# The raw projection weights issued on ScalarE's DMA queue in place of SP's, after the first 11 chunks

## The chip, the cores and the metric

One core of a Trainium2 chip. The metric is the device time of one execution in microseconds (us), the median of several runs. Instructions of five engines run side by side: PE (TensorE, matmuls; PEld is its weight load), DVE (VectorE), ACT (ScalarE), POOL (GpSimd) and SP (SyncE, which only issues DMAs). ACT and POOL can issue DMAs too. An engine takes its instructions strictly in the order in which they were written for it, so one that waits holds all behind it.

## The reference

A two-layer backbone over 2048 latent and 256 context tokens of width 1024, in fp32:

```python
xn = _rms_norm(x, g_norm) * (1 + sc) + sh          # sc, sh: silu(c) @ w_ada + b_ada
(au, av, az, bq, bk, bv, bz, cq, ck, cv, co, cz, cg) = _split_proj(xn @ w_in)
y_a = _gmlp_branch(au, av, az, w_s, b_s)           # chunks of 128 tokens
y_b = attention(q=bq, k=bk, v=bv) * silu(bz)       # 8 heads, 2 kv heads, rms norm and rope
y_c = sigmoid(co) * rms_norm(mlstm(cq, ck, cv, cg), both directions) * silu(cz)
x = x + gt * (concat([y_a, y_b, y_c]) @ w_out)
```

Context tokens go through the same weights. After the second layer a last RMSNorm follows.

## The kernel before

Tokens are tiled by 128: 18 tiles, 2 of context and 16 of latents. Each layer has a projection phase (`proj_phase`), an attention phase (`attn_phase`) and an output phase (`out_phase`). In the profile the projections run from 0 to about 890 us and from about 1740 to 2690 us.

**Projections.** The 18 tiles are taken in three macros of six. For each macro seven column groups (c1, c3, c2, a1, a2, b1, b2) are computed; for each group and tile, 8 contraction chunks times 3 matmuls (a weight and an input are each split in a high and a low part) add up in one PSUM bank: 24 matmuls. The normalized, split input of a tile is its `xn` (L465 to L487). After a tile's matmuls a post-processing generator of the group (`post_c1` to `post_b2`) takes the bank, mostly by ScalarE first.

**Weights.** A chunk is 128 rows of one group: 3 x 7 x 8 = 168 chunks in a layer. `wload` (L942) loads a chunk's raw fp32 into one of 3 buffers `raw`; `split_w` (L197) makes the split weight `w` from it: ScalarE copies (L199) and VectorE subtracts (L200), or, for every fourth chunk, GpSimd does both (L202, L203). `w` has 11 buffers, 8 for the group at work and 3 ahead. A `raw` buffer comes free with the subtraction; a `w` buffer with the last matmul that reads it.

**Queues.** `ld` (L50) issues on SP's queue (L53). All loads and nearly all stores go there; ScalarE issues the stores of c1 and c3 to scratch (L495, L518). Each DMA raises one of 8 semaphores, which all DMAs of SP and ACT take in turn, and a DMA waits until the one before it on its semaphore has landed.

**Modulations and tables.** The modulations of layer 1 and the gates `gt` are made during layer 0 as filler (`mod_job`): 64 blocks of `w_ada` go into 3 buffers `mst`, and VectorE adds them into `mkv` (L401, L403: two instructions a block); PE sums over partitions (L434, L443). The rope tables `tab` are loaded in `rope_mul`. Both loads stand under `with tc.issue_after(lastw[0])`: it puts each instruction that is issued on the same engine as `lastw[0]`, the raw load issued last, behind that load.

**mLSTM.** In the last macro of a layer the mLSTM's jobs run beside the projections (`ml_state`, `ml_out`): chains of small loads (`mkv`, `mst`, `xt<-snm`, `msc`), a few instructions, and stores (`sst`, `sy`), all on SP's queue.

**Order.** A scheduler orders each engine's instructions by a simulated timeline; the order in which the code traces them is the priority. So an instruction that may start earlier can be put ahead of others on its engine.

Of the kernel before, what the change touches and what calls it, by code (L numbers as in the profile page):

```python
# [35 lines left out]
def hybrid_kernel(ctx: ExitStack, tc: tile.TileContext, x, c, ctxt, c_ctx, w_ada, b_ada, g_norm, w_in, w_s, b_s,  # L36
                  gq, gk, b_gates, g_head, w_out, g_final, rope, out):
    nc = tc.nc
# [12 lines left out]
    def ld(dst, src):  # L51

        r = nc.sync.dma_start(dst, src)  # L53
        if gate[0] is not None:
            tc.add_manual_dep(r.ins, gate[0].name,
                              mybir.DependencyInfo(mybir.DependencyClass.NoSync, mybir.DependencyReason.DATA),
                              reason="order of the loads")
        return r

    def nm(s):  # L60
        uid[0] += 1
        return f"{s}_{uid[0]}"
# [242 lines left out]
    def proj_phase(l):  # L305
        with ExitStack() as st:
# [624 lines left out]
            for mi in range(NM):  # L931
                for gn, cols in groups:
                    for k in range(KC):
                        src, o = [], 0
# [4 lines left out]
            wt, wraw, lastw = [], [], [None]  # L939
            freed = [0]  # L940

            def wload():  # L942
                while len(wraw) < len(chunks) and len(wraw) < len(wt) + 3:
                    raw = rawp.tile([P, 512], F32, tag="raw", name=nm("raw"))
                    for (a, o, w) in chunks[len(wraw)][0]:
                        lastw[0] = ld(raw[:, o:o + w], a).ins
                    wraw.append(raw)

            def wtick(most=2):
                for _ in range(most):  # L950
                    j = len(wt)
                    if j >= len(chunks) or j >= freed[0] + 11:
                        break
                    wt.append(split_w(wraw[j], wring(), chunks[j][1], chunks[j][2] % 4 != 1))
                    wload()

            xgens = [make_xn(i, halves=first) for i in macros[0][:AHEAD]]
            if first:
                silu_prep()
                rT = mod_rows(0)  # L960
                mod_load(0, 0)
                for gen in xgens:
                    next(gen)
                    next(gen)
                mod_first(0, 0, rT)
                wload()
                mod_load(0, 1)
                for gen in xgens:
                    next(gen)
                    next(gen)  # L970
                wtick(4)
                mod_first(0, 1, rT)
                for gen in xgens:
                    run_all(gen)
                wtick(12)
                layer_params(0, k2(), k1(P)[0:4])
            else:
                with tc.high_priority(offset=140):
                    wload()
                    wtick(12)  # L980
                    for gen in xgens:
                        run_all(gen)
            for mi, mac in enumerate(macros):
                for gi, (gn, cols) in enumerate(groups):
# [8 lines left out]
                    for ii, i in enumerate(mac):  # L993
                        full = not (last and i < NCT)
                        ml = mi == NM - 1 and (gi >= 3 or gi == 2 and ii >= 1)
                        if i in todo:
                            acc = pacc()
                            c0, w = (0, n) if full or gn == "c3" else (256, 256)
# [291 lines left out]
```

## Time and profile before

| | |
|---|---|
| median of 3 runs | 3673.63 us (3672.63 to 3673.88) |
| the profiled execution | 3684.58 us, its span 3682.9 us |
| PE busy | 3582.6 us, 97% of the span |
| DVE, ACT, POOL busy | 2556.9 us (69%), 1942.0 us (53%), 1892.3 us (51%) |
| DMA moved | 359.21 MB, mean 98 GB/s |
| chain that ended last, by engine | PE 69%, DMA 6%, DVE 4%, POOL 3%, issue 2%, SP's queue 2%, ACT 2% |

The last row follows the end of the program back to what released each step. SP has no busy time in the profile, since issuing is not counted; its DMA issues stand in the timeline as SPq, and those of ScalarE as ACTq.

### The profile page before, as it was taken

How to read it: one execution, taken by the hardware profiler on the slowest of the kernel's cores; microseconds unless marked ns; L12 is line 12 of the kernel's file. 1: busy time of each engine (PE TensorE's matmuls, PEld its weight loads, DVE VectorE, ACT ScalarE, POOL GpSimd, SP SyncE). 2: the span in 40 equal slices, each digit the busy share in tenths (PEclk: the TensorE clock that was granted, in tenths of full speed). 3: DMA queues.
4: the chain of work that ended last, by engine and by line, in shares of the span. 5: the costliest groups of instructions: out<-in, count | busy, mean ns of one | idle time of the engine just before them, and what ended most of it. 6: DMA issues, size and time to landing. Idle time of an engine off the chain costs nothing.

```text
span 3682.9 us, 58371 instructions
## 1 busy us (share of the span) xinstructions
PE 3582.6 (97%) x19405; PEld 2937.3 (80%) x19405; DVE 2556.9 (69%) x6341; ACT 1942.0 (53%) x3409; POOL 1892.3 (51%) x2448
## 2 busy tenths in 40 slices
PE   8999999998999999999999999999999999999999
PEld 4877778776888888887788788877778888888787
DVE  4676664778888888887324636466888888888754
ACT  4223243334878788786114432432377877777621
POOL 2241342454777777776322524244557777777610
PEclk9999999999999999999999999999999999999999
DMA  7456455576001011002545553557720101100143
GB/s 216 137 138 175 138 129 136 159 194 156 25 28 37 17 35 43 24 12 95 175 121 151 132 148 83 141 145 180 174 57 18 31 27 35 35 24 10 58 148 113
DMA packets 531690, 359.21 MB, mean 98 GB/s; under 512 B 297274, under 2 KB 432178, under 8 KB 531388
## 3 DMA queue, kind: packets, MB, share of 16 engines
q1 hardware_dynamic: 518172, 336.05, 33.8%
q10 hardware_dynamic: 10368, 9.52, 0.8%
q0 software_dynamic: 2848, 9.91, 0.7%
q8 instruction: 154, 2.52, 0.3%
q14 instruction: 148, 1.21, 0.1%
HBM read 269.56 MB, written 85.76 MB: 96 GB/s over the span
## 4 chain that ended last, share of the span: by engine, by line
PE 69%; DMA 6%; DVE 4%; POOL 3%; issue 2%; SPq 2%; ACT 2%; DVEq 0%; POOLq 0%; ACTq 0%
PE acc L209 20%; PE m L1131 14%; PE acc L1096 14%; PE tr L1113 9%; PE x L209 6%; PE x L1113 4%; SPq L53 2%; DMA raw<-in_w_in_dram 1%; DMA xt<-snm 1%; DMA mkv<-sc 1%; DMA tab<-in_rope_dram 1%; DVE w L200 1%; DVE e L1098 1%; PE tr L476 0%; POOL pT L1120 0%
## 5 line engine op out<-in xcount | busy, mean ns | idle before, releaser
L209 PE MATMUL acc<-w,xn 128*128 128x512 f32 (+2 forms) x4728 | 1096.5, 385 | 5.3 <-POOL w L203 1.7
L209 PEld LDWEIGHTS acc<-w,xn 128*128 128x128 f32 x4728 | 844.2, 191 | 182.8 <-issue 5.4
L1098 DVE TENSOR_SCALAR_CACHE_REDUCE e<-acc,rqall 128x512 f32<-128x512 f32 (+1 forms) x1296 | 858.1, 690 | 144.4 <-PE acc L1096 76.6
L1131 PE MATMUL m<-pT,vst 128*128 128x512 f32 (+1 forms) x2336 | 775.3, 415 | 4.8 <-POOL pT L1120 4.0
L1096 PE MATMUL acc<-kst,qs 128*128 128x512 f32 (+1 forms) x2592 | 744.5, 385 | 11.6 <-DVE e L1098 10.0
L1120 POOL TENSOR_TENSOR pT<-pf,pT 128x512 fp32r<-128x512 f32 (+1 forms) x564 | 730.5, 1302 | 29.7
L1104 ACT ACTIVATE e<-e,nmx 128x2304 f32<-128x2304 f32 (+1 forms) x272 | 578.5, 2127 | 61.4 <-DVE nmx L1103 60.7
L1119 POOL TENSOR_SCALAR pT<-pf 128x512 fp32r<-128x512 f32 (+1 forms) x564 | 356.8, 636 | 338.5 <-ACT pf L1118 332.9
L1096 PEld LDWEIGHTS acc<-kst,qs 128*128 128x128 f32 x2592 | 447.4, 189 | 92.1 <-DVE e L1098 21.7
L1131 PEld LDWEIGHTS m<-pT,vst 128*128 128x128 f32 x2336 | 411.7, 189 | 65.6 <-POOL pT L1120 8.6
L1113 PE MATMUL tr<-ident,e 128*128 128x128 f32 x3084 | 456.9, 273 | 3.0 <-DVE pT L1123 2.1
L1113 PEld LDWEIGHTS tr<-ident,e 128*128 128x128 f32 x3084 | 375.1, 141 | 79.1 <-DVE pT L1123 4.0
L200 DVE TENSOR_TENSOR w<-raw,w 128x512 fp32r<-128x512 f32 (+1 forms) x276 | 205.5, 755 | 184.0 <-ACT w L199 182.3
L199 ACT CAST w<-raw 128x512 fp32r<-128x512 f32 (+1 forms) x276 | 161.6, 595 | 299.0 <-DMA raw<-in_w_in_dram 265.1
L1123 DVE TENSOR_TENSOR pT<-tr,pT 128x512 fp32r<-128x512 f32 x405 | 274.2, 683 | 59.5 <-ACT pT L1122 58.4
L209 PE MATMUL acc<-w,xs 128*128 128x512 f32 x1224 | 294.2, 398 | 1.7 <-DVE xs L249 1.3
L1122 ACT CAST pT<-tr 128x512 fp32r<-128x512 f32 x405 | 234.4, 587 | 95.2 <-PE tr L1113 79.8
L209 PEld LDWEIGHTS acc<-w,xs 128*128 128x128 f32 x1224 | 230.9, 189 | 58.3 <-DVE xs L249 1.7
L209 PE MATMUL x<-w,xn 128*128 128x512 f32 (+1 forms) x1128 | 263.3, 379 | 10.4 <-DVE w L200 6.0
L1118 ACT COPY pf<-tr 128x512 f32<-128x512 f32 (+1 forms) x372 | 214.5, 584 | 87.1 <-PE tr L1113 77.8
L202 POOL TENSOR_SCALAR w<-raw 128x512 fp32r<-128x512 f32 (+1 forms) x92 | 65.5, 712 | 361.7 <-PE acc L209 158.7
L209 PEld LDWEIGHTS x<-w,xn 128*128 128x128 f32 x1128 | 200.1, 190 | 54.8 <-DVE w L200 8.9
(282 smaller groups left out, 4402.9 us busy)
## 6 DMA issues: line engine op xcount, KB each, us to landing
raw<-in_w_in_dram SPq DMA_DIRECT2D x240, 256.0 KB, 3.1
raw<-in_w_in_dram SPq DMA_DIRECT2D x144, 128.0 KB, 2.4
mkv<-sc SPq DMA_DIRECT2D x68, 258.0 KB, 4.0
xt<-snm SPq DMA_DIRECT2D x68, 256.0 KB, 4.5
yr<-sy SPq DMA_DIRECT2D x34, 512.0 KB, 6.5
mst<-in_w_ada_dram SPq DMA_DIRECT2D x64, 256.0 KB, 3.7
qd<-sq SPq DMA_DIRECT2D x128, 128.0 KB, 2.8
xres<-xnew POOLq DMA_DIRECT2D x18, 512.0 KB, 5.2
```

What stands on the lines that cost most here:

```text
L200: V.tensor_tensor(wt[:, 1, :n], raw[:, :n], wt[:, 0, :n].bitcast(F32), op=ALU.subtract)
L209: T.matmul(acc[:, :n], xs[:, a, k, :], ws[k][:, b, c0:c0 + n], start=(k == 0 and j == 0), stop=(k == KC - 1 and j == 2))
L1096: T.matmul(acc[:, 0:w], u['qs'][:, r, j * P:(j + 1) * P], kf[:, c0:c0 + w], start=(r == 0), stop=(r == 1))
L1098: V.tensor_scalar(e[:, c0:c0 + w], acc[:, 0:w], rqall[:, u['tiles'][j], u['h']:u['h'] + 1], None, op0=ALU.mult, op1=ALU.max, accum_out=mx[ ...
L1104: A.activation(e[:, 0:nk], e[:, 0:nk], AF.Exp, bias=nmx, scale=1.0, accum_out=u['den'][:, j:j + 1])
L1113: T.transpose(tr[:, j * P:(j + 1) * P], u['e'][j][:, s * P:(s + 1) * P], ident)
L1118: A.copy(pf[:, 0:w], tr[:, 0:w])
L1119: G.tensor_scalar(pt_[:, 0, 0:w], pf[:, 0:w], 1.0, 0.0, op0=ALU.mult, op1=ALU.add)
L1120: G.tensor_tensor(pt_[:, 1, 0:w], pf[:, 0:w], pt_[:, 0, 0:w].bitcast(F32), op=ALU.subtract)
L1122: A.copy(pt_[:, 0, 0:w], tr[:, 0:w])
L1123: V.tensor_tensor(pt_[:, 1, 0:w], tr[:, 0:w], pt_[:, 0, 0:w].bitcast(F32), op=ALU.subtract)
L1131: T.matmul(u['o'][:, 0:w], vst[u['g']][:, s, :], pt_[:, r, 0:w], start=(s == 0 and r == 0), stop=(s == u['nk'] - 1 and r == 1))
```

## The change

From the 12th chunk of each layer on, the raw weights are issued by ScalarE:

```diff
             def wload():
                 while len(wraw) < len(chunks) and len(wraw) < len(wt) + 3:
+
+                    q = ld if len(wraw) < 11 else nc.scalar.dma_start
                     raw = rawp.tile([P, 512], F32, tag="raw", name=nm("raw"))
                     for (a, o, w) in chunks[len(wraw)][0]:
-                        lastw[0] = ld(raw[:, o:o + w], a).ins
+                        lastw[0] = q(raw[:, o:o + w], a).ins
                     wraw.append(raw)
```

Line numbers behind this place grow by 2, and the moved loads have L948. `lastw[0]` is now an instruction of ScalarE for all but the start, while the loads under `issue_after` stay on SP.

**VectorE at the start of layer 0**, behind the first half of the first three tiles' `xn` (xn_324, xn_333, xn_342). `mst` are blocks of `w_ada` for the filler, `mkv` its sums, `w` the split weights of the first groups:

```order
 L487 TENSOR_TENSOR xn_333<-xt_330,xn_333 128x512
 L487 TENSOR_TENSOR xn_342<-xt_339,xn_342 128x512
+L401 TENSOR_SCALAR mkv_975<-mst_977,silT 128x512
+L401 TENSOR_SCALAR mkv_976<-mst_977,silT 128x512
+L403 SCALAR_TENSOR_TENSOR mkv_975<-mst_979,silT,mkv_975 128x512
+L403 SCALAR_TENSOR_TENSOR mkv_976<-mst_979,silT,mkv_976 128x512
+L403 SCALAR_TENSOR_TENSOR mkv_975<-mst_1008,silT,mkv_975 128x512
+L403 SCALAR_TENSOR_TENSOR mkv_976<-mst_1008,silT,mkv_976 128x512
 L200 TENSOR_TENSOR w_462<-raw_450,w_462 128x512
 L200 TENSOR_TENSOR w_537<-raw_455,w_537 128x512
```

Sums of the filler, which stood behind the first two groups, now stand here. From this place to the last instruction of the three tiles' `xn` 29 of them were put in (25 of L403, 4 of L401).

**SP's queue at the same time**, behind the last block of `w_ada` for layer 0's own modulation (xn_411). `tab` are rope tables, `sst` the zero states of the mLSTM, `raw` the weights:

```order
 L53 DMA xn_411<-in_w_ada_dram 128x2x512 x2
+L53 DMA mst_977<-in_w_ada_dram 128x512
+L53 DMA mst_979<-in_w_ada_dram 128x512
+L53 DMA mst_1008<-in_w_ada_dram 128x512
+L53 DMA tab_1991<-in_rope_dram 128x128
+L53 DMA tab_2057<-in_rope_dram 128x128
+L53 DMA tab_2123<-in_rope_dram 128x128
 L53 DMA sst_0_176<-st_6002 128x130
 L53 DMA sst_1_195<-st_6010 128x130
```

Three blocks of the filler and three tables now go ahead of the rest of the first weights; further blocks stand between these.

**ScalarE at the change from group c2 to a1 in the first macro**, with what each row waits for (DMAHW are the 8 semaphores of SP's and ACT's DMAs). Before:

```order
98 L199 CAST w_1396<-raw_1174 128x512 [waits DMAHW1_49,DVE_49,PE_49]
99 L199 CAST w_1401<-raw_1179 128x512 [waits DMAHW2_49,PE_49,Pool_49]
100 L199 CAST w_1412<-raw_1399 128x512 [waits DMAHW5_49,DVE_49,PE_49]
101 L505 ACTIVATE k_222_1454<-acc_1379 128x512 [waits DVE_49,PE_49,Activation_49]
102 L199 CAST w_1430<-raw_1404 128x512 [waits DMAHW7_49]
103 L199 CAST w_1436<-raw_1409 128x512 [waits DMAHW1_49,DMAHW0_49,Pool_49]
```

And now:

```order
122 L199 CAST w_1396<-raw_1174 128x512 [waits DMAHW0_49,PE_49]
123 L199 CAST w_1401<-raw_1179 128x512 [waits DMAHW1_49,PE_49]
124 L948 DMA raw_1399<-in_w_in_dram 128x512 [waits DVE_49]
125 L948 DMA raw_1404<-in_w_in_dram 128x512 [waits DVE_49]
126 L199 CAST w_1412<-raw_1399 128x512 [waits DMAHW7_49,PE_49]
127 L948 DMA raw_1409<-in_w_in_dram 128x256 [waits DMAHW2_49,Pool_49]
128 L948 DMA raw_1409<-in_w_in_dram 128x256 [waits DMAHW3_49]
129 L505 ACTIVATE k_222_1454<-acc_1379 128x512 [waits PE_49]
130 L199 CAST w_1430<-raw_1404 128x512 [waits DMAHW1_49]
```

The raw loads, with their waits for VectorE, GpSimd and earlier DMAs, now stand between the copies, and ahead of the instruction L505 that takes a PSUM bank.

## Rows read from the trace of the kernel before

**Rows 1.** Stages of the span (start:end in us): length, busy time of PE, PEld, DVE, ACT, POOL with counts, granted clock of TensorE, busy share of the DMA engines, GB/s.

```profile
0.00:100.00 100.00, 86.46 (x368) 52.77 (x369) 44.24 (x97) 41.36 (x91) 22.98 (x52) 0.95 0.74 215
100.00:200.00 100.00, 95.52 (x451) 79.02 (x450) 68.25 (x132) 25.20 (x56) 28.80 (x36) 0.98 0.46 140
200.00:600.00 400.00, 382.75 (x1812) 312.49 (x1811) 242.88 (x512) 133.13 (x306) 135.01 (x190) 0.99 0.56 142
...
700.00:900.00 200.00, 181.49 (x1071) 142.69 (x1070) 154.04 (x419) 62.43 (x176) 97.60 (x138) 0.96 0.70 174
...
1900.00:2450.00 550.00, 546.69 (x2712) 452.27 (x2710) 277.26 (x622) 209.56 (x474) 192.38 (x278) 1.00 0.50 130
...
2500.00:2700.00 200.00, 184.70 (x1026) 143.65 (x1026) 158.40 (x426) 72.17 (x183) 90.12 (x124) 0.93 0.70 173
```

**Rows 2.** What PE waited for from 100 to 600 us, those waits that end with a split weight: total us, times, longest us.

```profile
PE x L209 <- DVE w L200: 6.0, 4, 1.8
PE x L209 <- ACT w L199: 3.9, 4, 2.2
...
PE acc L209 <- POOL w L203: 1.7, 1, 1.7
...
PE acc L209 <- ACT w L199: 1.1, 1, 1.1
```

**Rows 3.** What SP's queue waited for from 100 to 600 us, those that free a raw buffer: total us, times, longest.

```profile
SPq L53 <- DVE w L200: 59.6, 34, 19.7
...
SPq L53 <- POOL w L203: 23.0, 15, 2.8
```

**Rows 4.** SP's queue, a timeline from the last macro of layer 0.

```profile
749.84 1.33 SPq L53 DMA_DIRECT2D raw<-in_w_in_dram  x2
751.21 3.25 SPq L53 DMA_DIRECT2D sy<-k  x4
754.86 2.98 SPq L53 DMA_DIRECT2D sk<-k  x4
```

**Rows 5.** The longest waits for a DMA from 700 to 900 us: total us, times, longest.

```profile
POOL xt L797 <- DMA xt<-snm: 27.1, 12, 5.5
...
POOL m L764 <- DMA mkv<-sc: 18.5, 7, 4.9
```

**Rows 6.** The filler's instructions on `mst` from 30 to 500 us: count, duration in ns (min/median/max), first and last start; and the time from issue to landing of its loads.

```profile
L403 DVE SCALAR_TENSOR_TENSOR mkv<-mst,silT,mkv x98: 705/748/1793, 104.2 to 490.4; 128x512 f32<-128x512 f32 x98
...
L401 DVE TENSOR_SCALAR mkv<-mst,silT x14: 475/483/1515, 103.4 to 447.0; 128x512 f32<-128x512 f32 x14
...
DMA to landing us min/median/max: 2.6/3.7/3.8
```

**Rows 7.** Timeline of DVE at the start: start us, us, engine, line, operation, out<-in, shapes, count, and in brackets the idle time before and what ended it.

```profile
30.14 1.29 DVE L487 TENSOR_TENSOR xn<-xt,xn 128x512 fp32r<-128x512 f32 x2
36.90 1.35 DVE L200 TENSOR_TENSOR w<-raw,w 128x512 fp32r<-128x512 f32 x2 [5.46 <-ACT w L199]
...
52.55 0.16 DVE L362 TENSOR_TENSOR mod<-m,rT 128x4 f32<-128x4 f32 x1 [4.78 <-PE m L395]
...
58.47 0.69 DVE L487 TENSOR_TENSOR xn<-xt,xn 128x512 fp32r<-128x512 f32 x1 [0.32 <-ACT xn L486]
```

**Rows 8.** The stretch from 30 to 60 us, columns as in rows 1.

```profile
30.00:60.00 30.00, 29.59 (x106) 13.66 (x105) 9.01 (x22) 10.33 (x23) 4.38 (x5) 0.98 0.48 149
```

**Rows 9.** Timeline of ACT and of its DMA issues (ACTq) at the start.

```profile
36.25 1.28 ACT L199 CAST w<-raw 128x512 fp32r<-128x512 f32 x2 [5.54 <-DMA raw<-in_w_in_dram]
...
64.26 1.05 ACT L465 ACTIVATE xn<-xt 128x1024 fp32r<-128x1024 f32 x1
64.64 0.33 ACTq L495 DMA_DIRECT2D sc<-k  x1
```

**Rows 10.** Timeline of PE at the start, columns as in rows 7.

```profile
56.27 3.18 PE L209 MATMUL x<-w,xn 128*128 128x512 f32 x12
...
59.52 5.79 PE L209 MATMUL acc<-w,xn 128*128 128x512 f32 x24
...
68.31 1.66 PE L476 MATMUL tr<-ident,xt 128*128 128x128 f32 x8 [2.12 <-DVE xt L483]
```

**Rows 11.** Issues of raw loads on SP's queue in three stretches, columns as in rows 6: from 100 to 600, from 700 to 900 and from 2500 to 2700 us.

```profile
L53 SPq DMA_DIRECT2D raw<-in_w_in_dram x144: 327/358/1733, 112.7 to 592.8; - x144
...
L53 SPq DMA_DIRECT2D raw<-in_w_in_dram x12: 328/378/735, 699.8 to 837.5; - x12
...
L53 SPq DMA_DIRECT2D raw<-in_w_in_dram x10: 375/379/893, 2526.8 to 2618.6; - x10
```

**Rows 12.** One change of group: ACT's copies of two weights, DVE's first subtraction behind them, and SP's queue, from three timelines.

```profile
250.53 1.31 ACT L199 CAST w<-raw 128x512 fp32r<-128x512 f32 x2
...
258.93 0.67 DVE L200 TENSOR_TENSOR w<-raw,w 128x512 fp32r<-128x512 f32 x1
...
253.13 7.26 SPq L53 DMA_DIRECT2D sq<-k  x8
260.49 0.93 SPq L53 DMA_DIRECT2D raw<-in_w_in_dram  x2
```

**Rows 13.** What ACT waited for from 100 to 600 us, the longest.

```profile
ACT w L199 <- DMA raw<-in_w_in_dram: 101.1, 40, 8.6
```

## The prediction

> **What bounds the kernel now.** I read the stages first. TensorE is busy in 97% of the span, so nearly all that a change can win is TensorE's idle time, and all that it can lose is more of it. The stages show where that idle time lies [rows 1]: 13.5 us in the first 100 us; 4.5 us from 100 to 200 and 17.3 us from 200 to 600 us; 18.5 us from 700 to 900 and 15.3 us from 2500 to 2700 us, where the mLSTM runs beside the last macro of a layer and the granted clock is lower (0.96 and 0.93). From 1900 to 2450 us, layer 1's projections without the filler, only 3.3 us are idle. The attention phases issue no raw weight.
>
> Second, TensorE's waits: of the idle time from 100 to 600 us, 12.7 us end with a split weight (6.0 + 3.9 + 1.7 + 1.1) [rows 2]. These the change can reach directly.
>
> Third, SP's queue. From 100 to 600 us it stood 59.6 + 23.0 = 82.6 us at raw loads whose buffer was not yet free, 49 times [rows 3]. In the mLSTM's stretches it issues without a gap: three pieces in a row, ten issues, fill the time from 749.8 to 757.8 us [rows 4], and the engines wait there for loads that it issues late (27.1 and 18.5 us on GpSimd) [rows 5].
>
> **The change part by part.** The profiled execution took 3684.6 us, 11 us above the median of 3673.6; I make the sum against the former and carry the difference over to the latter.
>
> *The start: +7 us (0 to +10).* The filler's loads lose their place behind the raw loads, since `issue_after` binds only instructions of the engine that issued the raw one, and so they and their sums move to the start. The sums cost VectorE 25 x 0.75 + 4 x 0.48 = 20.7 us [rows 6], between 31.4 us (end of the first halves of `xn`) and 59.2 us (end of the second halves) [rows 7]. VectorE is busy for only 9.0 us from 30 to 60 us [rows 8], so on paper there is room. But the first 5 us of it can't be used: nothing of weights lands before 36.2 us, behind the blocks of `w_ada` [rows 9], and the added loads queue there too. From 36.3 us on, 20.7 + 7.7 us of work end at 64.7 us, 5.5 us after the old end; and since only three `mst` buffers exist and a load takes 3.7 us to land [rows 6], I add 1.5 us for sums that stand at the head of VectorE with no data. TensorE starts the second halves at 56.3 us, as soon as their first `xn` is there, and 2.1 us of waiting soon follow [rows 10]; with nothing else in its order it waits all 7 us. If the sums fitted into the gap before 52.6 us [rows 7] it would be nothing; with the clock that idle time costs, 10 us.
>
> *100 to 200 us: -3 us (-4.5 to 0).* What VectorE has done early it needn't do here. At best all idle time of the stretch goes (4.5 us) [rows 1].
>
> *Weights at a change of group, layer 0: -5 us (-12.7 to 0).* Raw loads no longer stand behind stores. That helps where SP was late, not where the buffer was: of 144 issues [rows 11] SP stood waiting at 49 [rows 3], and in one change of group the subtraction frees a buffer at 259.6 us, after 8 stores had held SP from 253.1 to 260.4 us, and the load goes at 260.5 [rows 12]: SP cost 0.9 us, VectorE, 7 us behind ScalarE's copies, the rest. I take less than half of 12.7.
>
> *The mLSTM's stretches: -6 us (-15 to 0).* SP loses 12 and 10 of its issues there, at a median of 0.38 us: 8 us in all, if the stretch is as long as SP's work [rows 11]; at 0.67 us, as two of them took in the timeline, 15 us [rows 4]. TensorE has 18.5 and 15.3 us of idle time to give back [rows 1], so even the bound can be paid; but the chains wait for landings too, so I take some three quarters of the 8.
>
> *ScalarE: +2 us (0 to +14).* An issue itself costs it nothing: a DMA went out from 64.64 to 64.97 us while an activation ran from 64.26 to 65.31 [rows 9]. But the 82.6 us of waiting [rows 3] move to it, and behind a blocked load stand copies of weights and the instructions that take PSUM banks. Most of it is covered: ScalarE already stood 101.1 us, up to 8.6 us at a time, for raw weights to land [rows 13], and TensorE has other banks to fill, at 5.8 us a tile [rows 10]. Only a wait longer than a tile reaches it; the longest, 19.7 us, would by 14 us.
>
> *Layer 1's projections between, and the attention: 0*, since TensorE is idle for 3.3 us in 550 [rows 1], and no raw load is issued in attention. If ScalarE's lead were lost there, the price would be that of the line above again.
>
> Sum: 7 - 3 - 5 - 6 + 2 = -5 us: 3679.6 in place of 3684.6, so 3668.6 for the median, which I give as 3669. About 0.2% (7 us) is what a measurement of this kernel can tell from no change, so the forecast lies within it.
>
> **A rule against it.** A raw load takes SP some 0.36 us to issue [rows 11]. The Trainium skill, "DMA: Bandwidth & Descriptors", section "Issuing engines are not separate DMA queues", says that DMAs of several issuing engines run on the same 16 DMA engines, and that a second one saves only the time of initiating them, usually small. The rows agree that an issue is small, but a queue in order holds back what is behind a wait as well, which that sentence doesn't count; the rival that takes only the issue time is the third below.
>
> **The rivals.**
> - *SP was the bound everywhere it was full (28%).* The weights' stalls go by 12 us, the mLSTM's stretches give 9, VectorE's relief gives 3, and the start costs 3. That is -21 us, 3653. For it: SP's gapless issues [rows 4]. Against: the subtraction at 259 us was late without SP [rows 12].
> - *ScalarE holds (23%).* In order behind a load whose buffer is not free, it delays the copy of the next weight and the emptying of banks; it decides once a wait outlasts a tile (5.8 us) at several of the six changes of group a macro. Start +10, ScalarE +14, the mLSTM's stretches only -3, weights 0: +21 us, 3695. For it: waits of up to 19.7 us [rows 3]. Against: ScalarE waits at these places already [rows 13].
> - *Moved, not freed (12%).* The order gives many moved loads a wait for a DMA semaphore too, and SP's stores take those in turn; a raw load then still waits for stores, only on another engine, and no more than issue time is saved. Weights 0, the mLSTM's stretches -6, ScalarE +5, the start +7 and -1 after it: +5 us, 3679.
>
> **How the numbers follow.** My forecast has 37%, with a range of its own of -12 to +5 us; a third of it is beyond -7. Faster by over 0.2%: 28 + 12 = 40%. Slower by over 0.2%: 23% and a third of the third rival (4%), 27%. Within 0.2%: the remaining 33%. The range of 8 in 10 takes in most of both outer cases: 3648 to 3692.
>
> **What would show it.** Right: TensorE's second halves start some 7 us later than 56.3 us, with sums on `mst` in VectorE's timeline from 35 us on; SP's waits for subtractions gone from 100 to 600 us and found at ScalarE's queue; fewer idle us of TensorE from 700 to 900 and 2500 to 2700 us. Wrong: the old start; idle time of TensorE in front of its weights as before or more; new idle time from 1900 to 2450 us, which would be ScalarE's; or mLSTM's stretches as long as before with SP's issues still gapless.

## The result, and the profile after

| | before | after |
|---|---|---|
| median | 3673.76 us (6 runs, 3672.12 to 3681.51) | 3651.76 us (6 runs, 3645.43 to 3658.06) |
| ratio, 95% interval | | 0.9927 [0.9916, 0.9938] |
| the profiled execution | 3684.58 us | 3652.97 us |
| PE busy | 3582.6 us (97%) | 3575.4 us (98%) |
| chain that ended last, PE's share | 69% | 77% |
| moved by SP's and ScalarE's queues (q1, q10) | 336.05 and 9.52 MB | 258.87 and 86.69 MB |

Faster by 0.73% [0.62, 0.84]; the medians lie 22 us apart, and the ratio makes it 27 us [23, 31]. The forecast was no change (3669), so it was wrong; the time lies within the range. Below, "us by the ratio" is (1 - ratio) x 3676, and an interval in square brackets behind it is made from the ratio's in the same way.

To see where the time went, both traces are cut at the same instructions of ScalarE: the first on c3 (96.9 us before, 103.4 after), on c1 in the third macro (559.2 and 539.3) and on c3 there (592.0 and 569.2); the last on b2 in layer 0 (891.0 and 866.7); the first on c3 in layer 1's last macro (2384.4 and 2355.1); the last on b2 (2677.9 and 2645.9). Before, columns as in [rows 1]:

```profile
0.00:96.90 96.90, 83.36 (x344) 49.67 (x345) 43.12 (x93) 40.25 (x89) 22.98 (x52) 0.95 0.73 216
96.90:559.20 462.30, 440.57 (x2049) 358.20 (x2048) 302.94 (x622) 151.79 (x348) 160.49 (x216) 0.99 0.54 143
...
592.00:891.00 299.00, 282.30 (x1680) 226.08 (x1679) 214.63 (x586) 102.07 (x277) 141.65 (x198) 0.97 0.64 169
2384.40:2677.90 293.50, 282.62 (x1626) 225.27 (x1625) 206.53 (x557) 97.17 (x260) 136.19 (x191) 0.95 0.64 164
```

After:

```profile
0.00:103.40 103.40, 88.11 (x350) 52.55 (x351) 65.87 (x129) 40.39 (x88) 24.88 (x55) 0.90 0.84 252
103.40:539.30 435.90, 432.57 (x2049) 356.21 (x2048) 276.68 (x583) 151.75 (x342) 160.71 (x217) 1.00 0.54 141
...
569.20:866.70 297.50, 286.05 (x1695) 229.09 (x1693) 212.66 (x590) 101.81 (x277) 139.29 (x196) 0.95 0.66 170
2355.10:2645.90 290.80, 280.49 (x1633) 222.89 (x1631) 202.89 (x557) 96.93 (x260) 136.04 (x189) 0.95 0.64 166
```

Read the second row of each: as many matmuls (2049), 26.4 us shorter. 18.4 of these are idle time of TensorE (length less busy: 21.7 before, 3.3 after). The other 8.0 are busy time: the mean granted clock went from 0.99 to 1.00 (1.00 is the upper level, 2.4 GHz), and the matmuls took 440.6 and then 432.6 us. They are not quite the same ones: 16 of the filler's (L434) have moved to the start, and 16 more of L209 stand here.

| stretch | forecast | seen |
|---|---|---|
| start, to c3's first tile | +7 | +6.5 |
| from there to the third macro | -3 and -5 | -26.4 |
| one group more | 0 | -2.9 |
| the mLSTM's stretches | -6 | -1.5 and -2.7 |
| between them (layer 0's attention and output, layer 1's projections) | 0 | -5.0 |
| behind the projections | 0 | -0.8 |
| sum | -5 | -32.8 |

The sum is that of the two profiled executions, and the one before was 11 us above its median; the medians have -22. So some of these us, in the long row too, are that execution's and not the change's (e10 below, which is nearly the kernel before, shows how much may be: its middle is 8 us shorter, its time 4). Against e10's middle, 454.3 us with 437.3 of them busy, the change gains 18.4 us: 13.7 of idle time and 4.7 of busy time.

The long row's waits. Before, what TensorE waited for from 96.9 to 559.2 us (its four longest with a split weight stand in [rows 2]):

```profile
PE m L567 <- DVE asv L553: 2.1, 2, 1.1
PE tr L476 <- DVE rT L355: 2.0, 1, 2.0
...
PE m L434 <- DVE asv L572: 1.1, 1, 1.1
...
PE tr L353 <- DVE xt L483: 1.0, 1, 1.0
PE tr L476 <- DVE xt L468: 1.0, 1, 1.0
PE tr L476 <- DVE xt L483: 0.9, 1, 0.9
PE acc L209 <- DVE w L200: 0.9, 2, 0.7
```

With [rows 2] these make 13.6 us for split weights and 8.1 us for other results of VectorE. After, from 103.4 to 539.3 us, this is the whole list:

```profile
PE x L209 <- DVE w L200: 2.3, 2, 2.0
PE acc L209 <- ACT w L199: 1.0, 2, 0.8
```

VectorE's own waits for the filler's blocks in the same stretch, before:

```profile
DVE mkv L403 <- DMA mst<-in_w_ada_dram: 30.4, 22, 3.6
...
DVE mkv L401 <- DMA mst<-in_w_ada_dram: 9.7, 4, 4.3
```

After, beside ScalarE's wait for raw weights (95.6 us before, cut alike; [rows 13] is the wider window) and SP's longest:

```profile
DVE mkv L403 <- DMA mst<-in_w_ada_dram: 10.6, 10, 4.6
```

```profile
ACT w L199 <- DMA raw<-in_w_in_dram: 64.9, 35, 5.6
```

```profile
SPq L53 <- DMA raw<-in_w_in_dram: 56.2, 9, 29.3
```

So two things became earlier: the filler's blocks, for which VectorE had stood 40.1 us, and the raw weights. SP's waits of [rows 3] are all but gone (2.6 us); in their place SP stands for raw loads of ScalarE that hold a shared semaphore. TensorE's whole list is 3.3 us, so little can have come of that.

### The profile page after: what moved, and what is told of

It reads as the page before. It is cut to its first block, busy times and chain, and to the rows that moved or that the text cites. A ratio compares the mean times of both kernels' runs of the same rounds, so it can differ in the third digit from the quotient of the medians.

```text
span 3650.1 us, 58250 instructions
## 1 busy us (share of the span) xinstructions
PE 3575.4 (98%) x19405; PEld 2933.3 (80%) x19405; DVE 2551.3 (70%) x6341; ACT 1943.4 (53%) x3409; POOL 1890.3 (52%) x2448
## 3 DMA queue, kind: packets, MB, share of 16 engines
q1 hardware_dynamic: 459996, 258.87, 26.3%
q10 hardware_dynamic: 68544, 86.69, 8.4%
## 4 chain that ended last, share of the span: by engine, by line
PE 77%; DVE 5%; DMA 5%; POOL 2%; ACT 2%; issue 2%; SPq 1%; ACTq 0%; DVEq 0%; POOLq 0%
PE acc L209 27%; PE m L1133 14%; PE acc L1098 14%; PE tr L1115 9%; PE x L209 7%; PE x L1115 4%; DMA raw<-in_w_in_dram 1%; DMA xt<-snm 1%; SPq L53 1%; DVE e L1100 1%; DVE w L200 1%; PE m L777 1%; DMA xt<-in_x_dram 1%; PE tr L476 0%; POOL pT L1122 0%
## 5 line engine op out<-in xcount | busy, mean ns | idle before, releaser
L209 PE MATMUL acc<-w,xn 128*128 128x512 f32 (+2 forms) x4728 | 1096.7, 385 | 2.0 <-ACT w L199 1.0
L209 PEld LDWEIGHTS acc<-w,xn 128*128 128x128 f32 x4728 | 843.6, 191 | 179.7 <-issue 4.2
L209 PE MATMUL acc<-w,xs 128*128 128x512 f32 x1224 | 292.5, 396 | 0.0
L209 PEld LDWEIGHTS acc<-w,xs 128*128 128x128 f32 x1224 | 229.7, 188 | 56.1 <-ACT w L199 0.4
L209 PE MATMUL x<-w,xn 128*128 128x512 f32 (+1 forms) x1128 | 263.2, 380 | 3.9 <-DVE w L200 2.3
L1115 PE MATMUL x<-ident,e 128*128 128x128 f32 x1556 | 235.5, 273 | 3.4 <-DVE pT L1125 3.0
```

Source lines behind the costliest of these rows:

```text
L209: T.matmul(acc[:, :n], xs[:, a, k, :], ws[k][:, b, c0:c0 + n], start=(k == 0 and j == 0), stop=(k == KC - 1 and j == 2))
L1115: T.transpose(tr[:, j * P:(j + 1) * P], u['e'][j][:, s * P:(s + 1) * P], ident)
```

## Theories and experiments

**Theory Q**: the gain is that of the raw loads, which no longer queue on SP. **Theory T**: it is that of the lost ties; the filler's loads no longer stand behind raw loads. Each of the first four kernels has one without the other. All were run beside the kernel before.

**e1**, the kernel before without both ties:

```diff
-                    with tc.issue_after(lastw[0]):
-                        ld(raw[:, 0:512], w_ada[l, ...
+                    ld(raw[:, 0:512], w_ada[l, ...
...
-                with tc.issue_after(lastw[0]):
-                    ld(tab, rope[:, i - NCT])
+                ld(tab, rope[:, i - NCT])
```

> Raw weights stay on SP's queue; only the two issue_after ties (filler blocks of w_ada, rope tables) are taken away, so both groups of loads may go ahead of raw loads. Theory Q (the gain from 100 to 540 us comes from the raw loads leaving SP's queue): the start loses its 8 us as in the changed kernel and little comes back, about 3675 to 3680 us. Theory T (the gain comes from the ties being lost: filler blocks come earlier, VectorE no longer stands at sums without data): start +8, middle -29, about 3652 to 3658 us.

**e2**, the change with the ties kept in the scheduler's order, across the engines:

```diff
-                    with tc.issue_after(lastw[0]):
-                        ld(raw[:, 0:512], w_ada[l, ...
+                    r = ld(raw[:, 0:512], w_ada[l, ...
+                    tc.add_manual_dep(r.ins, lastw[0].name, <NoSync>, ...)
```

(and the same for `tab`).

> Raw weights on ScalarE's queue as in the change, but the ties are kept by an order edge across engines, so the filler stays behind the weights of the start and is not moved there. Theory Q: gain of the middle kept, loss of the start gone, about 3642 to 3648 us. Theory T: no gain of the middle, only what the mLSTM's stretches give, 3666 to 3674 us.

**e3** is the change, **e4** the kernel before, both with the ties behind the 11th chunk's raw load alone:

```diff
                         lastw[0] = q(raw[:, o:o + w], a).ins
+                        if len(wraw) < 11:
+                            firstw[0] = lastw[0]
...
-                with tc.issue_after(lastw[0]):
+                with tc.issue_after(firstw[0]):
```

> The change, with the filler's and the tables' loads tied behind the last raw load on SP (the 11th chunk) alone, so that they can't go into the start but are free after it. Both theories: the 8 us of the start come back, about 3644 us; if the sums at the start were what relieved VectorE later, the middle gives back as much and it stays near 3652.

> All raw weights on SP; ties only behind the 11th chunk, as in the run before this one. Theory Q: no gain, 3670 to 3676 us. Theory T: the middle's gain without the start's loss, 3645 to 3650 us.

Measured, with the later kernels. "Start" and "middle" are shifts of the two cuts 96.9 and 559.2 against before; "waits for mst" are VectorE's from 97 to 560 us; idle time is TensorE's between the two cuts, less by the waits for split weights ("w") and for other results.

| | raw on | ratio [95%] | median us | start | middle | waits for mst | idle: w + other |
|---|---|---|---|---|---|---|---|
| before | SP | 1 | | 0 | 0 | 40.1 | 13.6 + 8.1 |
| change | ACT | 0.9927 [0.9916, 0.9938] | 3651.76 | +6.5 | -19.9 | 10.6 | 3.3 + 0 |
| e1 | SP | 0.9955 [0.9940, 0.9969] | 3661.35 | +10.0 | -20.3 | 12.6 | 3.9 + 0 |
| e2 | ACT | 0.9931 [0.9910, 0.9952] | 3654.30 | -3.5 | -23.0 | 24.6 | 3.0 + 3.4 |
| e3 | ACT | 0.9920 [0.9902, 0.9937] | 3648.48 | +6.0 | -15.3 | 9.9 | 3.6 + 2.2 |
| e4 | SP | 0.9929 [0.9908, 0.9949] | 3654.59 | +6.1 | -22.6 | 13.3 | 2.1 + 0.9 |
| e5 | SP | 0.9949 [0.9934, 0.9964] | 3657.13 | +0.7 | -20.4 | 0 | 7.2 + 1.3 |
| e6 | SP | 0.9943 [0.9928, 0.9957] | 3655.59 | +4.1 | -19.1 | 11.8 | 6.5 + 0.6 |
| e7 | SP | 0.9973 [0.9963, 0.9983] | 3668.02 | -1.4 | -11.7 | 41.1 | 7.6 + 6.1 |
| e8 | ACT | 0.9923 [0.9908, 0.9938] | 3648.38 | -0.5 | -18.0 | 19.7 | 6.7 + 2.4 |
| e9 | SP | 0.9930 [0.9918, 0.9942] | 3652.20 | -0.5 | -23.4 | 0 | 5.0 + 0.9 |
| e10 | SP | 0.9990 [0.9980, 0.9999] | 3670.58 | -1.6 | -9.7 | 40.3 | 11.7 + 5.3 |
| e11 | ACT | 0.9948 [0.9934, 0.9962] | 3658.25 | -3.0 | -21.3 | 20.3 | 3.0 + 4.5 |
| e12 | ACT | 0.9931 [0.9919, 0.9943] | 3654.23 | -1.9 | -22.4 | 0 | 2.5 + 2.2 |

The two cuts don't enclose the same work in every kernel. Of L209's matmuls 1844 lie between them before, 1860 in the change, 1831 in e1, 1868 in e2 and 1865 in e4, at 0.23 us each. So a few us in the columns "start" and "middle" can be the cut's.

Both theories fall as they stood. From the first cut to the second the change gains 26.4 us; without the ties and with every raw load on SP it is 30.3 (e1) and 28.7 us (e4), and with the raw loads on ScalarE and the filler kept behind them 19.5 us (e2). For as much work as before these would be some 28, 25, 30 and 25 us (estimates, from the counts and durations of TensorE's instructions between the cuts). By the ratio e1 gave 17 us [11, 22], e2 25 [18, 33], e3 29 [23, 36] and e4 26 [19, 34]: theory Q allowed e1 and e4 nothing, theory T allowed e2 at most the mLSTM's part. Either edit is enough. e3 and e4 were also to bring the start back, and did not: the 35 sums ran there all the same.

That led to **theory C**, a cycle: SP stands at a raw load whose buffer VectorE frees; the filler's load stands behind it; VectorE stands at the sum that waits for that load. Two pieces of it can be read in the kernel before, from two timelines, SP's and VectorE's:

```profile
402.64 3.26 SPq L53 DMA_DIRECT2D raw<-in_w_in_dram  x4
...
406.72 2.76 SPq L53 DMA_DIRECT2D raw<-in_w_in_dram  x4
409.53 3.96 SPq L53 DMA_DIRECT2D mst<-in_w_ada_dram  x4
```

```profile
407.96 0.69 DVE L200 TENSOR_TENSOR w<-raw,w 128x512 fp32r<-128x512 f32 x1 [2.42 <-ACT w L199]
...
412.38 0.75 DVE L403 SCALAR_TENSOR_TENSOR mkv<-mst,silT,mkv 128x512 f32<-128x512 f32 x1 [2.03 <-DMA mst<-in_w_ada_dram]
```

Eight issues of raw loads go out between 402.6 and 409.5 us, and SP stands 2.5 us in them, until a buffer is free or, by the profile's naming, until VectorE's instruction right behind a subtraction is done. The filler's block follows at 409.5, and VectorE stands 2.0 us until it has landed. Some 25 us later ten issues take 10.4 us, where [rows 11] has 0.36 us for one, and VectorE's sum waits for the block behind them:

```profile
432.68 10.41 SPq L53 DMA_DIRECT2D raw<-in_w_in_dram  x10
443.15 0.42 SPq L53 DMA_DIRECT2D mst<-in_w_ada_dram  x1
```

```profile
447.00 0.49 DVE L401 TENSOR_SCALAR mkv<-mst,silT 128x512 f32<-128x512 f32 x1 [1.31 <-DMA mst<-in_w_ada_dram]
```

e5 to e8 take this apart.

**e5**: the sums read `mfix`, a block of `w_ada` that is there from the start, and keep their places in VectorE's order (in the change 35 of the 112 had moved to the start):

```diff
-                    mod_sum(accs, raw[:, 0:512], k)
+                    was = mod_sum(accs, mfix[:, 0:512], k)
+                    for q in was:
+                        tc.add_manual_dep(q.ins, raw.ins.name, <NoSync>, ...)
```

> The kernel before, raw loads on SP and all ties kept; only the filler's sums on VectorE read a block of w_ada that was loaded once at the start, in place of the block that their own load brings (the loads are still issued, in the same places; the sums keep their places in VectorE's order; so the gates and layer 1's modulations come from one repeated block). What is gone is VectorE's wait for those loads to land. Theory C (a cycle: SP stands at a raw load whose buffer VectorE frees, the filler's load stands behind it, and VectorE stands at the sum that waits for that load): VectorE's 40 us of waiting from 97 to 560 us go, TensorE's idle time there falls from 22 to under 6 us, and the time is 20 to 34 us below the kernel before, with no loss at the start. Theory Q (the raw loads come late because they queue behind stores on SP, whatever VectorE waits for): at most 6 us are gained, since SP's queue is as it was. Theory W (VectorE has too much to do in these groups, and the change helped by moving 35 sums to the start): no gain either, since no sum is moved.

19 us by the ratio [13, 24], just short of the lower end, though in the middle theory C's terms hold: 21 us there (-20.4 and +0.7), no loss at the start. TensorE's idle time fell from 21.7 to 8.5 us (under 6 was expected):

```profile
97.60:538.80 441.20, 432.69 (x2051) 354.22 (x2051) 296.19 (x622) 151.92 (x348) 162.84 (x216) 1.00 0.56 150
```

VectorE's standing at these loads is thus a cause, worth most of the change's middle by itself (21 of 26 us, or 13 of 18 against e10's), and Q and W fall: in SP's order each of the filler's 64 loads stands behind as many issues of raw loads as before, and no sum has moved. But the cycle does not close. SP still stands 66.4 and 21.5 us at raw loads for VectorE's and GpSimd's subtractions (58.8 and 21.5 before, cut alike), and ScalarE still waits 89.6 us for raw weights (95.6 before); only GpSimd's wait for them fell, from 55.8 to 31.1 us, while 19.5 us at the same line are now put down to a store. What VectorE held up were its own results: TensorE's waits for VectorE fell from 15.0 to 2.7 us, those for split weights of ScalarE and GpSimd only from 6.7 to 5.8.

**e6** removes only the filler's tie, **e7** only the tables' (the two halves of e1's diff).

> The kernel before with one of the two ties gone: the filler's loads are no longer held behind the raw load issued last; the rope tables still are. All raw loads stay on SP. 35 sums move to the start. Theory C: nearly all of what both ties together gave (17 us), so 12 to 22 us below the kernel before, with the start 5 us later and VectorE's waits for these loads from 40 to about 12 us. If the tables' tie were the one that mattered: within 4 us of the kernel before.

> The kernel before with the other tie gone: the rope tables' loads are free, the filler's loads still stand behind the raw load issued last. No sum of the filler moves. Theory C: within 5 us of the kernel before, VectorE still waits some 40 us for the filler's loads. If the tables' tie were the one that mattered: 12 to 22 us below.

e6 gave 21 us [16, 27], as theory C said. e7 gave 10 us [6, 14], twice what it allowed, with VectorE's waits unchanged at 41.1 us: the tables' loads behind raw loads seem to cost something of their own. Its one profile can't show what: its middle is 10.3 us shorter, but e10's is 8.0 us shorter too. GpSimd's wait for tables fell from 21.8 to 11.4 us, but in the change it is 24.1 and in e9, without that tie too, 21.2; how the tables reach TensorE stays open.

**e8**, the change with 24 in place of 11, and the ties of e3 behind the 24th chunk:

> The change with two numbers moved: the raw loads go to ScalarE from the 25th chunk on in place of the 12th, and the filler's and the tables' loads are held behind the 24th chunk's raw load. It is meant to keep the gain of the middle (26 us from 97 to 559) without the start's loss (6.5 to 8.7 us). Theory C, and the start's loss coming from the 35 moved sums: the start as in the kernel before, the middle as in the change, so 3 to 9 us below the change. If the sums that come behind the 24th chunk then delay the weights there as much: the same time as the change, within 4 us.

The start is as before (-0.5), so its loss is that of the sums that moved; with them behind the 11th chunk (e3, e4) it stayed. The middle gained less (18 us in place of 26), so of the 3 to 9 us below the change that were expected 1.5 are left by the ratio, within the intervals.

The last four ask whether the holds add up, and for a version that is better than both.

**e9** is e5 without the tables' tie; **e12** is e2 with e5's sums.

> The kernel before, raw loads on SP, with two things gone at once: VectorE's waits for the filler's loads (as in the run where the sums read one block that was loaded once; gates and layer 1's modulations come from that block) and the tie of the rope tables' loads. If the change's gain is the sum of these two holds of SP's queue (22 us and 11 us when each was taken away alone), 28 to 36 us below the kernel before. If the two are the same idle time twice, as two ways to free VectorE: 20 to 26 us. If 14 of the change's 26 us came from the raw loads' own place on SP, it stays well above the change: under 18 us.

> The same order and queues as in the run with raw loads on ScalarE and the ties kept in order only, but the filler's sums read the block that was loaded once, so VectorE waits for none of the filler's loads (gates and layer 1's modulations come from that block). Beside the run on SP with those waits gone (22 us below the kernel before) it shows what the raw loads' move to ScalarE is worth when VectorE is not held. Theory C: little, 0 to 8 us more (the tables' loads leave the raw loads too), so 22 to 30 us below the kernel before. If the place of the raw loads mattered by itself: 12 us more or better, 34 us or more below.

e9: 26 us [21, 30], the middle 22.9. 19 and 10 would be 29, which the interval just holds. Against a sum speaks the idle time: e5 has 8.5 us left, e9 5.9, so they are mostly the same us. e12: 25 us [21, 30], 7 more than e5 by the ratio, but the intervals overlap, and the medians lie 22 us below the kernel before in both. The raw loads' move does what it says even when VectorE is never held: ScalarE waits 69.9 us for raw weights (89.6 in e5), TensorE 2.5 us for split weights in place of 7.2. That it wins time there is not shown: e9, with every raw load on SP and the tables free as in e12, gained as much.

The change does two things at once: it frees the filler's loads, and it takes the raw loads out of SP's order. Since either is enough (e6; e2, in which VectorE still stands 24.6 us), no share of its gain can be given to one of them.

**e10**, the kernel before with the filler's loads two ahead, **e11**, e2 with the same:

```diff
-                nxt = load(0)
+                nxt = [load(0), load(1)]
...
-                    raw = nxt
-                    if k + 1 < KC:
-                        nxt = load(k + 1)
+                    raw = nxt.pop(0)
+                    if k + 2 < KC:
+                        nxt.append(load(k + 2))
```

> The kernel before with one number changed: the filler loads its blocks two ahead of the sum in place of one ahead (its three buffers allow it). Raw loads on SP, all ties kept, every sum in its place. Theory C: a block is asked for one step earlier, so VectorE waits 10 to 25 us for them in place of 40 from 97 to 560 us, and 6 to 16 us are won. If SP's hold is longer than a step of the filler, or the third buffer comes free too late: within 5 us of the kernel before.

> A candidate for the best version: raw loads on ScalarE's queue from the 12th chunk on as in the change; the filler's and the tables' loads are kept behind the raw loads in the scheduler's order only (no waiting on the chip), so that no sum moves to the start; and the filler loads two ahead. Theory C: the start as before, VectorE's waits for the filler under 15 us in place of 25 (one ahead), so 27 to 35 us below the kernel before and 2 to 8 us below the change. If the waits that were left cost TensorE nothing: the same as with one ahead, 25 us below the kernel before.

Theory C missed in both. In e10 VectorE's waits are those of the kernel before to 0.2 us:

```profile
DVE mkv L403 <- DMA mst<-in_w_ada_dram: 29.9, 19, 4.3
DVE mkv L401 <- DMA mst<-in_w_ada_dram: 10.4, 5, 3.7
```

The lead hardly reaches SP's order: 52 of the filler's 64 loads stand behind exactly as many issues of raw loads as before, the other 12 behind 4 to 14 fewer. Of the lead, nothing arrives in VectorE's waits; 4 us [0, 7] by the ratio. e11 is no better than e2 (19 and 25 us).

Of the versions that compute the whole, e3 and e8 have the lowest ratios, 0.9920 and 0.9923; the change's 0.9927 lies in the intervals of both, so none is shown to beat it.

## Why the prediction was wrong, by its steps

- **The start, +7: the number right, +6.5, the working in part.** VectorE's busy time there rose by 22.8 us (20.7 in the prediction), by the sums; e8 and e2, which leave the sums where they were, lose nothing there. But I let TensorE wait all 7 us, and its idle time rose by 1.8 us only. 4.7 us are busy time at a granted clock of 0.90 in place of 0.95, with 16 matmuls of the filler (L434, 1.8 us) moved here and 10 fewer of L209. That the size came out is partly luck. Here VectorE stands at the first block, where I had left 5 us empty, and TensorE finds its `xt` 1.5 and 2.4 us late:

```profile
35.86 0.88 DVE L401 TENSOR_SCALAR mkv<-mst,silT 128x512 f32<-128x512 f32 x2 [4.92 <-DMA mst<-in_w_ada_dram]
```

```profile
58.44 0.66 PE L476 MATMUL tr<-ident,xt 128*128 128x128 f32 x4 [1.53 <-DVE xt L483]
...
75.64 0.65 PE L476 MATMUL tr<-ident,xt 128*128 128x128 f32 x4 [2.41 <-DVE xt L483]
```

- **The step that failed: "weights at a change of group: -5 (-12.7 to 0)", with "100 to 200 us: -3".** -26.4 was measured for both, outside even their bounds together (-17.2); against e10's middle it is -18.4. Three things were wrong in it. First, I asked which waits of TensorE name a split weight and left out the 8.1 us that it waited for other results of VectorE, though [rows 1] gave 4.5 + 17.3 = 21.8 us of idle time. Second, I took VectorE's lateness [rows 12] as VectorE's own and did not open the list of what VectorE waits for, where 40.1 us for the filler's loads stand; what those loads had queued behind is in SP's order. e5 and e6 show that this alone was worth about 20 us (19 and 21 by the ratio). Third, the prediction had a price for the clock where idle time was added, at the start, and none where it was taken away: 8.0 us of busy time, 4.7 against e10.
- The place of [rows 12] was a bad witness besides. In the change the copy there starts at 247.77 us and the subtraction still at 256.47, 8.7 us later; the gain is spread over all groups of the stretch.
- **The mLSTM's stretches, -6: -4.2, but not shown to be SP's.** In the first, idle time fell from 16.7 to 11.4 us, and busy time rose by 3.7 with 15 matmuls more (granted clock 0.97, then 0.95). GpSimd's longest wait of [rows 5], 27.1 us in all, is now 21.7. But both stretches together, 592.5 us before and 588.3 after, take 584.9 us in e10 and 585.5 in e4, where SP issues every raw load: what shortened them needs no move.
- **ScalarE, +2 (0 to +14): at most that.** The mechanism is there, at the same change of group, from ScalarE's timeline:

```profile
247.77 1.31 ACT L199 CAST w<-raw 128x512 fp32r<-128x512 f32 x2
...
257.18 1.83 ACTq L948 DMA_DIRECT2D raw<-in_w_in_dram  x2
259.13 0.60 ACT L634 ACTIVATE k<-acc 128x512 f32<-128x512 f32 x1 [10.05 <-PE tr L476]
```

  ScalarE stands 8 us ahead of a raw load until the subtraction of 256.47 us frees its buffer, and L634, which takes a PSUM bank, starts after 10 us of idle time, 12 us behind the one before it, where 5.5 us lay between the three before. So it is some 6.5 us late, longer than a tile (5.8 us), and still TensorE is idle for only 2.3 us in the 81 us around it. In the whole middle it waits 1.0 us for ScalarE.
- **Layer 1's projections: 0, right in kind**: they had little idle time to give, and the shift grows from -25.8 to -29.3 us in them. Layer 1 has no filler, so VectorE can't be held by it there.
- **The rivals.** "SP was the bound everywhere" (-21) came nearest in its total and in naming VectorE's relief, but split it wrongly (12 for weights, 9 for the mLSTM, 3 for VectorE). "ScalarE holds" needed banks that TensorE did not lack. "Moved, not freed" was right that the shared semaphores tie the two queues, but had raw loads wait for SP's stores; what the trace shows is SP standing for raw loads (56.2 us). Its price, +5 us in all, did not come.

Open: how the tables' tie costs 10 us [6, 14]; and why e2 and e12, without a loss at the start, measure no better than the change: their intervals overlap with its own, so nothing here tells a smaller gain from chance.

## What to carry to other kernels

Before you call an engine late, open the list of what it waited for itself; a late producer in an in-order queue two steps back shows up as lateness of everything that the held engine makes. Bound a change by the idle time of the stretch, and by the clock that goes with it, not by the waits that carry the name of what is moved. When a queue mixes loads that wait for a buffer with loads that could go at once, take either kind off it. Here which one mattered little, and an earlier request did not help, since it left most loads at their place behind the blocked ones.

## What was not expected of the hardware

SP and ScalarE take 8 DMA semaphores in turn, so that SP stood 56.2 us in the middle, once 29.3 us, for raw loads that ScalarE had issued, and 178.1 us in the whole span: two queues, but not two independent ones. And the clock went with the idle time in both directions. 18.4 us less idle time came with 8.0 us less busy time for as many matmuls (13.7 with 4.7 against e10), at a granted clock of 1.00 in place of 0.99; 1.8 us more at the start came with 4.7 us more busy time, at 0.90 in place of 0.95. That the one brings the other about is not shown here.
